# A 256-token hybrid decoder layer: low parts in whole blocks, one product moved forward, attention heads begun later

## The chip, the cores and the metric

The kernel runs on one NeuronCore of a Trainium2 chip. The core has a matmul engine (TensorE, PE in the rows; PEld is its loading of the stationary operand), a vector engine (VectorE, DVE), an activation engine (ScalarE, ACT), GpSimd (POOL) and SyncE (SP), which here only issues DMAs. The engines run side by side; each takes its own instructions in the order in which they were written and waits for the others through semaphores. The metric is the device time of one execution in microseconds (us).

## The reference, cut to what matters

One layer, 256 tokens, width 2048, float32. One wide projection feeds four causal attention branches of 4 heads each; every branch output is gated, projected, weighted with a sigmoid gate and summed; one output projection follows, then a norm.

```python
h = rms_norm(x, norm_w)
p = h @ w_in                     # (256, 2048) @ (2048, 17492)
(z, gate, dsa_qkv, idx_q, idx_k, idx_w, fox_qkv, fox_f, diff_qkv, dil_qkv) = jnp.split(p, IN_OFFSETS, axis=-1)
# four branches b, 4 heads of 128 each: softmax attention with a bias per head and pair of positions
#   0 top-k sparse (an indexer picks 64 keys), 1 forgetting, 2 difference of two softmaxes, 3 dilated
for b in range(N_BRANCHES):
    y = branches[b].reshape(bsz, seq, BRANCH_WIDTH) * jax.nn.silu(z_parts[b])
    term = jax.nn.sigmoid(g_parts[b]) * (y @ w_branch[b])
    merged = term if merged is None else merged + term
return x + merged @ w_out        # then a final rms_norm
```

## The kernel before, in words

**Numbers.** Every float32 operand of a matmul is split into a high part, rounded to the engine's faster float32 format, and a low part, the rest. One product of a 128x128 activation tile with 512 weight columns is three matmuls (`three`, L378 to L380): activation high by weight high, activation low by weight high, activation high by weight low.

**Units.** The weights pass through in units: a block of 512 rows by 512 columns (1 MB), loaded by SP into one of six raw slots. ACT copies it into `whi` (`split_hi`, L207), DVE subtracts into `wlo` (`split_lo`, L220), each in two halves of 128x1024, and PE runs 24 matmuls on it (12 where only one of the two 128-token halves is wanted). `whi` has 8 half buffers, `wlo` 6. The loop at the end of `body` writes the order: at each half of unit i it first writes the low part of the half that lies 5 halves ahead and the high part of the half that lies 7 ahead, then the unit's own matmuls. So when unit i ends, the low parts of two and a half later units have been written in DVE's queue, and the high parts of three and a half in ACT's. Only what stands behind them in a queue can be held up by them, and they by what stands ahead.

**Seven products.** A 2048 x 1024 stretch of `w_in` is done by `seven`: for one half of the rows (four blocks B11, B12, B21, B22) seven products P1 to P7 take the place of eight, with sums of blocks formed by DVE in place (`plus`, L187, three for each seven) and one by an accumulating DMA that POOL issues (`plus_dram`, L191: B12 + B11). P5 is the product that reads this accumulated sum. The other half of the rows is plain (units c2a, c2b, c1a, c1b). P units have 12 matmuls, c units 24. The order of the eleven units is a string: before, `P1 P3 P5 c2a P6 c2b P7 P2 c1a P4 c1b`. Four PSUM banks (X, Y, Z, W) take the sums; between products ACT and DVE read them out (classes `Tok` and `Gate`: p1, p5, u3 and c21 on ACT, u2, c12, c22 and c11 on DVE; in `Gate` a sigmoid on ACT follows). P5 goes alone into W, is read out by ACT (p5, L540), and only then may c2a write W again. c2a writes Z first (half of each half unit), then W.

**Stages.** After the indexer's projection come four branches, in the order 3, 2, 0, 1. A branch is: the seven of q and k (`ps_qk`), the seven of z and v (`ps_zv`), two sevens of gates (`ps_g`, called first and second gate here), and four units of the branch projection (`ps_b`). A merge and the output projection (`ps_o`) end the kernel.

**Threads.** The attention is written as generators that take one step after a unit, when enough units have passed (`pace`): `qk_thread` turns q and k on PE, `z_thread` forms silu(z) (a sigmoid on ACT, L625, and a product on DVE, L626) and turns it, `index_thread` scores and picks keys, and a `head_thread` or `diff_thread` for each of the 4 heads: logits on PE (L786), bias and maximum on DVE (L798 to L803), exponentials on ACT (L805); a step later the reciprocal on DVE; then the scaling on ACT (`scaled`, L821); then the transposes on PE (L812 to L814) with their copy `pt` on ACT (L816); one step later the product with v on PE (L876); then the output `y` and its high and low parts. The logits tile `lg` has three buffers, held from the logits until the transposes. Before, the four heads start with `qk_thread`, wait in `ready` until that has ended, and the first two (one for branch 2) go ahead while z and v are still being projected; the rest wait until `z_thread` has come to its turning. An instruction of a thread stands in its engine's queue between the `whi` or `wlo` of two units.

## Time and profile before

| | us |
|---|---|
| three runs, median (lowest to highest) | 1042.16 (1042.02 to 1044.82) |
| the profiled execution, its own time | 1044.16 |
| its span in the trace | 1042.4 |
| PE busy | 973.3 |
| DVE busy | 822.7 |
| ACT busy | 634.7 |
| mean granted clock of PE | 0.966 |

The span runs from the first to the last instruction of the trace; the time of the execution has 1.76 us more around it. A wait is put down to the engine and line that released it. "Idle before" in square brackets is the time in which the engine stood still ahead of that instruction. A granted clock of 1.00 is 2.4 GHz, 0.50 is 1.2 GHz. Stages are cut at the first matmul of each seven.

### The profile page before, as it was taken

How to read it: one execution, taken by the hardware profiler on the slowest of the kernel's cores; microseconds unless marked ns; L12 is line 12 of the kernel's file. 1: busy time of each engine (PE TensorE's matmuls, PEld its weight loads, DVE VectorE, ACT ScalarE, POOL GpSimd, SP SyncE). 2: the span in 40 equal slices, each digit the busy share in tenths (PEclk: the TensorE clock that was granted, in tenths of full speed). 3: DMA queues.
4: the chain of work that ended last, by engine and by line, in shares of the span. 5: the costliest groups of instructions: out<-in, count | busy, mean ns of one | idle time of the engine just before them, and what ended most of it. 6: DMA issues, size and time to landing. Idle time of an engine off the chain costs nothing. (4 is left out here: it accounts for less than half of the span.)

```text
span 1042.4 us, 12131 instructions
## 1 busy us (share of the span) xinstructions
PE 973.3 (93%) x4443; PEld 799.7 (77%) x4443; DVE 822.7 (79%) x967; ACT 634.7 (61%) x834; POOL 73.0 (7%) x84
## 2 busy tenths in 40 slices
PE   9988998999999989989999979799999797999897
PEld 8866886878878867778788858688788686887776
DVE  5888899978697877597888775887987767869992
ACT  5756676686456667676555665863666567544641
POOL 2011010000010000021100000001000000010220
PEclk9998999999999999989999989899999898999998
DMA  9949484747876938159895574388958562788132
GB/s 321 293 112 286 155 252 136 221 143 243 261 228 228 290 102 242 41 197 280 209 303 161 203 201 162 122 256 222 302 176 275 162 202 81 259 271 317 58 144 81
DMA packets 109019, 213.64 MB, mean 205 GB/s; under 512 B 8083, under 2 KB 10293, under 8 KB 108576
## 3 DMA queue, kind: packets, MB, share of 16 engines
q1 hardware_dynamic: 96240, 181.06, 50.1%
q0 software_dynamic: 12688, 31.80, 14.9%
q8 instruction: 35, 0.57, 0.2%
q14 instruction: 24, 0.20, 0.1%
q10 hardware_dynamic: 32, 0.01, 0.0%
HBM read 204.44 MB, written 8.41 MB: 204 GB/s over the span
## 5 line engine op out<-in xcount | busy, mean ns | idle before, releaser
L207 ACT ACTIVATE whi<-raw 128x1024 fp32r<-128x1024 f32 (+1 forms) x439 | 448.9, 1051 | 238.2 <-DVE raw L187 81.0
L220 DVE TENSOR_TENSOR wlo<-raw,whi 128x1024 fp32r<-128x1024 f32 (+1 forms) x439 | 525.6, 1224 | 84.3 <-PE ps_g L380 21.4
L378 PE MATMUL ps_g<-whi,hT 128*128 128x512 f32 x352 | 145.9, 415 | 25.9 <-ACT g L540 25.9
L380 PE MATMUL ps_g<-wlo,hT 128*128 128x512 f32 x352 | 141.9, 403 | 0.4 <-DVE wlo L220 0.4
L379 PE MATMUL ps_g<-whi,hT 128*128 128x512 f32 x352 | 142.2, 404 | 0.0
L187 DVE TENSOR_TENSOR raw<-raw 128x2048 f32<-128x2048 f32 x51 | 117.8, 2310 | 1.1
L378 PEld LDWEIGHTS ps_g<-whi,hT 128*128 128x128 f32 x352 | 69.6, 198 | 44.2 <-ACT g L540 28.4
L380 PEld LDWEIGHTS ps_g<-wlo,hT 128*128 128x128 f32 x352 | 69.1, 196 | 16.0 <-DVE wlo L220 0.8
L379 PEld LDWEIGHTS ps_g<-whi,hT 128*128 128x128 f32 x352 | 69.4, 197 | 14.0
L378 PE MATMUL ps_qk<-whi,hT 128*128 128x512 f32 x176 | 70.3, 399 | 6.9 <-ACT tok L540 6.9
L380 PE MATMUL ps_qk<-wlo,hT 128*128 128x512 f32 x176 | 69.5, 395 | 1.8 <-DVE wlo L220 1.8
L378 PE MATMUL ps_zv<-whi,hT 128*128 128x512 f32 x176 | 70.5, 400 | 0.5 <-ACT v L540 0.5
L379 PE MATMUL ps_qk<-whi,hT 128*128 128x512 f32 x176 | 69.6, 395 | 0.0
L380 PE MATMUL ps_zv<-wlo,hT 128*128 128x512 f32 x176 | 68.7, 390 | 0.0
L379 PE MATMUL ps_zv<-whi,hT 128*128 128x512 f32 x176 | 68.6, 390 | 0.0
L191 POOL DMA_DIRECT2D raw<-in_w_in_dram x16 | 21.1, 1316 | 503.5 <-DMA raw<-in_w_in_dram 191.1
L380 PE MATMUL ps_g<-wlo,sf 128*128 128x512 f32 x128 | 50.5, 395 | 2.3 <-DVE wlo L220 2.3
L378 PE MATMUL ps_g<-whi,sf 128*128 128x512 f32 x128 | 51.6, 403 | 0.0
L379 PE MATMUL ps_g<-whi,sf 128*128 128x512 f32 x128 | 50.3, 393 | 0.0
L378 PE MATMUL ps_b<-whi,yT 128*128 128x512 f32 x128 | 49.9, 390 | 0.0
L380 PE MATMUL ps_b<-wlo,yT 128*128 128x512 f32 x128 | 49.8, 389 | 0.0
L379 PE MATMUL ps_b<-whi,yT 128*128 128x512 f32 x128 | 49.8, 389 | 0.0
(266 smaller groups left out, 1567.3 us busy)
## 6 DMA issues: line engine op xcount, KB each, us to landing
raw<-in_w_in_dram SPq DMA_DIRECT2D x132, 1024.0 KB, 6.4
raw<-in_w_in_dram POOLq DMA_DIRECT2D x16, 1024.0 KB, 11.3
raw<-in_w_branch_dram SPq DMA_DIRECT2D x16, 1024.0 KB, 5.2
raw<-in_w_out_dram SPq DMA_DIRECT2D x16, 1024.0 KB, 5.8
md<-g POOLq DMA_DIRECT2D x12, 512.0 KB, 5.3
raw<-in_w_in_dram SPq DMA_DIRECT2D x7, 512.0 KB, 9.8
xs<-in_x_dram SPq DMA_DIRECT2D x8, 256.0 KB, 8.1
mp<-md POOLq DMA_DIRECT2D x4, 512.0 KB, 8.7
```

The costliest lines, as they stand in the source:

```text
L187: nc.vector.tensor_tensor(to.tile, of.tile, to.tile, op=op)
L191: nc.gpsimd.dma_start(to.tile.rearrange("p (k n) -> p k n", k=of.nk), of.src[of.k0 * P:(of.k0 + of.nk) * P, of.c0:of.c0 + of.n] .rearrange ...
L207: nc.scalar.activation(u.parts[0][h][:, s_], raw[:, s_], AF.Copy)
L220: nc.vector.tensor_tensor(u.parts[1][h][:, s_], raw[:, s_], u.parts[0][h][:, s_].bitcast(F32), op=ALU.subtract)
L378: nc.tensor.matmul(ps, ahi, u.hi(k)[:, cols], start=first, stop=False, skip_group_check=on)
L379: nc.tensor.matmul(ps, alo, u.hi(k)[:, cols], start=False, stop=False, skip_group_check=on)
L380: nc.tensor.matmul(ps, ahi, u.lo(k)[:, cols], start=False, stop=last, skip_group_check=on)
```

## The change

Five things are edited.

- `whi` and `wlo` become whole-block tiles (128x2048, 4 and 3 buffers: the same room). ACT still writes the high part in two halves; the low part of both halves is one DVE operation of 128x2048 (211 of them; the first units and the kept block of the end keep halves).
- The loop writes the high part of unit i+3 (both halves) and the low part of unit i+2 (at its first half) while unit i runs. When unit i ends, the low parts of two later units and the high parts of three stand in the queues.
- The order of a seven becomes `P1 P5 P3 c2a ...`; in the first one `P1 P2 P5 P3 c2a ...`.
- The head threads start together with `z_thread`, at the end of the z and v seven, whose last unit (c1b) now needs the q and k turning and the constants (and for branch 0 the indexer) to be done. Head h takes its first step 2h steps later than head 0. Between the transposes and the product with v stand two steps instead of one; in `diff_thread` one step less lies between the norm and its transposes.
- The pace of branch 2's last 22 units goes from 15 to 14.

```diff
 def split_hi ...
-                u.parts[0][h] = wp.tile([P, 1024], F32R, name="whi", tag="whi", bufs=HI)[:, :n_]
+                if h == 0:
+                    u.high = wp.tile([P, 2048], F32R, name="whi", tag="whi", bufs=HI // 2)
+                u.parts[0][h] = u.high[:, h * n_:(h + 1) * n_]
 def split_lo ...
+        both = kept is None and h == 1 and u.parts[1][0] is None
...
+        if both:
+            nc.vector.tensor_tensor(u.low[:, :2 * n_], u.raw.tile[:, :2 * n_],
+                                    u.high[:, :2 * n_].bitcast(F32), op=ALU.subtract)
+            parts = 0
 def seven ...
-              order="P1 P3 P5 c2a P6 c2b P7 P2 c1a P4 c1b", s0=0):
+              order="P1 P5 P3 c2a P6 c2b P7 P2 c1a P4 c1b", s0=0):
 def qkvz_units ...
-                      start=[("qk", qk_thread)] + start, **(dict(
-                          need={"P1": ["stack"], "P3": ["forms"]},
-                          order="P1 P2 P3 P5 c2a P6 c2b P7 c1a P4 c1b") if b == FIRST else {}))
+                      start=[("qk", qk_thread)], **(dict(
+                          need={"P1": ["stack"], "P5": ["forms"]},
+                          order="P1 P2 P5 P3 c2a P6 c2b P7 c1a P4 c1b") if b == FIRST else {}))
-                        "ps_zv", need={"c1b": ["qk"]}, start=[("z", z_thread)]))
+                        "ps_zv", need={"c1b": ["qk", "fox", "const"] + ["index"] * (b == 0)},
+                        start=[z_thread] + start))
 def head_thread ...   (diff_thread alike)
-        yield from ready(b, h, 2)
+        for _ in range(2 * h):
+            yield
...
-        yield from values(b)
         yield
         pt = transposed(e)
         yield
+        yield
         o = att_ps("o")
...
-            u.pace = 15 if b == 2 else 18
+            u.pace = 14 if b == 2 else 18
 def low ...
-        if i < len(units):
+        if i < len(units) and (h or kept(units[i]) is not None):
 main loop ...
             low(2 * i + h + LO - 1)
-            high(2 * i + h + HI - 1)
+            high(2 * i + h + HI - 2)
             u.mm(u, h)
```

What this moves, at three places. First, ACT's queue at the first gate of branch 0, from the read-out of P1 (L537) to just behind that of P5 (L540); `sg` is the sigmoid of z, `lg,sm` the exponentials of a head. Before:

```order
L537 ACTIVATE g<-ps_g,rst 128x512
L207 ACTIVATE whi<-raw 128x1024 x2
L821 ACTIVATE lg<-lg,sm 128x128
L821 ACTIVATE lg<-lg,sm 128x256
L805 ACTIVATE lg,sm<-lg,mx 128x128
L805 ACTIVATE lg,sm<-lg,mx 128x256
L625 ACT_TABLE_LOAD
L625 ACTIVATE sg<-tok 128x1024
L207 ACTIVATE whi<-raw 128x1024 x2
L540 ACTIVATE g<-ps_g,rst 128x512
```

The same place after (line numbers of the changed kernel are ten higher: L547 is p1, L550 p5, L635 the sigmoid, L815 the exponentials):

```order
L547 ACTIVATE g<-ps_g,rst 128x512
L209 ACTIVATE whi<-raw 128x1024 x2
L550 ACTIVATE g<-ps_g,rst 128x512
L635 ACTIVATE sg<-tok 128x1024
L815 ACT_TABLE_LOAD
L815 ACTIVATE lg,sm<-lg,mx 128x128
L815 ACTIVATE lg,sm<-lg,mx 128x256
L209 ACTIVATE whi<-raw 128x1024 x6
```

P5's read-out stood behind a scaling, two exponentials, a sigmoid with its table and four halves of `whi`; now two halves stand ahead of it. Second, DVE's queue at the same place, from z's last read-out (L562) on. Before (behind these rows come a head's bias and maximum, and only then z's product with its sigmoid, L626):

```order
L562 SCALAR_TENSOR_TENSOR tok<-ps_zv,rst,tok 128x512
L866 RECIPROCAL sm<-sm 128x2
L220 TENSOR_TENSOR wlo<-raw,whi 128x1024
L187 TENSOR_TENSOR raw<-raw 128x2048
L220 TENSOR_TENSOR wlo<-raw,whi 128x1024 x2
L187 TENSOR_TENSOR raw<-raw 128x2048
L220 TENSOR_TENSOR wlo<-raw,whi 128x1024
```

After, up to the same product (L636):

```order
L572 SCALAR_TENSOR_TENSOR tok<-ps_zv,rst,tok 128x512
L225 TENSOR_TENSOR wlo<-raw,whi 128x2048 x2
L187 TENSOR_TENSOR raw<-raw 128x2048
L636 TENSOR_TENSOR tok<-tok,sg 128x1024
```

The halves are gone, and a sum of blocks stands behind a whole low part. Third, ACT's queue at the end of the same first gate, from the sigmoid of c22 to the read-out of the second gate's P1. Before (`pt` is the copy of the transposes):

```order
L576 ACTIVATE g<-g 128x512
L207 ACTIVATE whi<-raw 128x1024 x2
L821 ACTIVATE lg<-lg,sm 128x128
L821 ACTIVATE lg<-lg,sm 128x256
L805 ACT_TABLE_LOAD
L805 ACTIVATE lg,sm<-lg,mx 128x128
L805 ACTIVATE lg,sm<-lg,mx 128x256
L207 ACTIVATE whi<-raw 128x1024 x4
L580 ACT_TABLE_LOAD
L580 ACTIVATE g<-g 128x512
L583 ACTIVATE g<-ps_g,rst 128x512
L816 ACTIVATE pt<-ptp 128x384 x3
```

After, the end of that stretch (L826 is `pt`, L831 the scaling, L590 the sigmoid of c11):

```order
L826 ACTIVATE pt<-ptp 128x384
L209 ACTIVATE whi<-raw 128x1024 x4
L590 ACT_TABLE_LOAD
L590 ACTIVATE g<-g 128x512
L593 ACTIVATE g<-ps_g,rst 128x512
L842 ACTIVATE yT<-y 128x256
L831 ACTIVATE lg<-lg,sm 128x128
L831 ACTIVATE lg<-lg,sm 128x256
L815 ACT_TABLE_LOAD
L815 ACTIVATE lg,sm<-lg,mx 128x128
L815 ACTIVATE lg,sm<-lg,mx 128x256
```

Three copies of transposes stood in a row; now one comes at a time, and a head's scaling and another head's exponentials stand behind the sigmoid of c11. Over the whole program ACT has 28 table loads instead of 30; no other count changes but that of the low parts.

## Rows read from the trace of the kernel before

**Rows 1.** The page, part 1: busy time, share and instructions of each engine.

```profile
PE 973.3 (93%) x4443; PEld 799.7 (77%) x4443; DVE 822.7 (79%) x967; ACT 634.7 (61%) x834; POOL 73.0 (7%) x84
```

**Rows 2.** Waits of PE, whole span: us in total, times, longest us.

```profile
PE ps_g L378 <- ACT g L540: 25.9, 6, 6.5
PE o L876 <- ACT pt L816: 14.6, 4, 6.7
PE ps_qk L378 <- ACT tok L540: 6.9, 4, 4.1
PE ps_qk L380 <- DVE wlo L220: 3.6, 3, 1.8
```

**Rows 3.** Windows by stage: length, busy of each engine (instructions), PEclk, DMA share, GB/s.

```profile
60.23:119.41 59.18, 51.56 (x233) 40.39 (x231) 49.98 (x70) 36.40 (x47) 3.34 (x5) 0.94 0.60 183
...
166.63:221.56 54.93, 49.33 (x220) 40.36 (x218) 47.71 (x93) 37.24 (x57) 1.34 (x1) 0.94 0.57 173
...
374.85:432.11 57.26, 52.17 (x225) 40.38 (x225) 40.38 (x70) 38.94 (x59) 1.30 (x1) 0.94 0.55 166
432.11:487.18 55.07, 49.40 (x213) 40.37 (x213) 44.92 (x58) 39.80 (x68) 9.90 (x9) 0.91 0.59 183
...
509.03:551.07 42.04, 41.10 (x181) 33.71 (x180) 36.02 (x30) 24.36 (x25) 2.98 (x3) 1.00 0.84 252
...
594.70:648.62 53.92, 47.41 (x210) 38.92 (x209) 34.46 (x43) 31.33 (x44) 1.29 (x1) 0.94 0.58 176
648.62:702.85 54.23, 47.16 (x202) 38.53 (x201) 44.59 (x49) 37.61 (x50) 1.29 (x1) 0.91 0.57 178
...
810.27:863.50 53.23, 47.50 (x210) 39.00 (x209) 33.07 (x40) 31.34 (x44) 1.28 (x1) 0.94 0.59 178
863.50:915.77 52.27, 45.70 (x202) 37.69 (x201) 43.75 (x46) 37.38 (x50) 0.00 (x0) 0.93 0.57 197
```

**Rows 4.** Windows, an even stretch and one behind a wait of PE.

```profile
240.00:250.00 10.00, 10.00 (x46) 8.29 (x45) 9.77 (x11) 5.24 (x8) 0.00 (x0) 1.00 0.64 223
...
611.60:616.60 5.00, 5.00 (x12) 3.94 (x13) 3.40 (x4) 1.93 (x2) 0.00 (x0) 0.50 1.06 218
```

**Rows 5.** Timeline, branch 0's first gate, ACT and PE: start, us, what [idle before].

```profile
606.71 1.28 ACT L625 ACT_TABLE_LOAD   x1
608.00 1.06 ACT L625 ACTIVATE sg<-tok 128x1024 f32<-128x1024 f32 x1
...
610.86 0.67 ACT L540 ACTIVATE g<-ps_g,rst 128x512 f32<-128x512 f32 x1
...
611.58 0.79 PE L378 MATMUL ps_g<-whi,hT 128*128 128x512 f32 x1 [6.51 <-ACT g L540]
```

**Rows 6.** Timeline, where branch 0's second gate begins: DVE, ACT and PE.

```profile
648.25 0.29 DVE L798 TENSOR_TENSOR lg<-lps,bias 128x128 f32<-128x128 f32 x1 [10.61 <-PE ptp L814]
...
656.05 1.28 ACT L580 ACT_TABLE_LOAD   x1
657.35 0.63 ACT L580 ACTIVATE g<-g 128x512 f32<-128x512 f32 x1
657.88 0.67 ACT L583 ACTIVATE g<-ps_g,rst 128x512 f32<-128x512 f32 x1
...
658.98 1.22 PE L876 MATMUL o<-pt,v 128*128 128x256 f32 x2 [6.72 <-ACT pt L816]
```

**Rows 7.** Timeline, PE in branch 0's q and k.

```profile
519.66 0.50 PE L378 MATMUL ps_qk<-whi,hT 128*128 128x512 f32 x1 [0.94 <-ACT tok L540]
```

**Rows 8.** Groups by line on DVE, and a pair of low halves in the timeline.

```profile
L220 DVE TENSOR_TENSOR wlo<-raw,whi 128x1024 fp32r<-128x1024 f32 (+1 forms) x439 | 525.6, 1224 | 84.3 <-PE ps_g L380 21.4 <-issue 20.5 <-PE ps_qk L380 11.0
L187 DVE TENSOR_TENSOR raw<-raw 128x2048 f32<-128x2048 f32 x51 | 117.8, 2310 | 1.1
...
649.80 2.35 DVE L220 TENSOR_TENSOR wlo<-raw,whi 128x1024 fp32r<-128x1024 f32 x2
```

**Rows 9.** Waits of ACT, whole span: us in total, times, longest us.

```profile
ACT whi L207 <- DVE raw L187: 81.0, 30, 5.1
```

More of the change, by code (lines that the diff above doesn't have):

```diff
@@ L210, in split_lo @@
         n_ = u.nk // 2 * u.n
+        both = kept is None and h == 1 and u.parts[1][0] is None
         if not part:
             if kept is None:
-                u.parts[1][h] = wp.tile([P, 1024], F32R, name="wlo", tag="wlo", bufs=LO)[:, :n_]
+                if h == 0 or both:
+                    u.low = wp.tile([P, 2048], F32R, name="wlo", tag="wlo", bufs=LO // 2)
+                for i in range(0 if both else h, h + 1):
+                    u.parts[1][i] = u.low[:, i * n_:(i + 1) * n_]
             else:
@@ L629, in z_thread @@
             V["sz"] = at.tile([P, 4, S], F32, name="sz", tag="sz")
-            V["v of"] = b
             yield from turn(z_, V["sz"], 0)
@@ L833, in put_y @@
         nc.vector.tensor_tensor(yT[:, h, 1], y, yT[:, h, 0].bitcast(F32), op=ALU.subtract)
-    def ready(b, h, early):
-        while any(a[0] in ("qk", "index", "fox", "const") for a in active):
-            yield
-        if h < early:
-            for _ in range(2 * h):
-                yield
-        else:
-            while V.get("v of") != b:
-                yield
-            for _ in range(h - early):
-                yield
-                yield
-    def values(b):
-        while V.get("v of") != b or any(a[0] == "z" for a in active):
-            yield
     def head_thread(b, h):
@@ L882, in diff_thread @@
             V["yT"] = big.tile([P, 4, 2, S], F32R, name="yT", tag="y")
-        yield from ready(b, h, 1)
+        for _ in range(2 * h):
+            yield
         er = []
@@ L899, in diff_thread @@
         yield
-        yield from values(b)
         yield
@@ L922, in diff_thread @@
                                     op0=ALU.mult, op1=ALU.mult)
-        yield
         yield
@@ L1248, in low @@
         i, h = divmod(q, 2)
-        if i < len(units):
+        if i < len(units) and (h or kept(units[i]) is not None):
             split_lo(units[i], h, kept(units[i]))
-    for q in range(2 * RAMP + 1, 2 * RAMP + HI - 1):
+    for q in range(2 * RAMP + 1, 2 * RAMP + HI - 2):
         high(q)
```

## The prediction

> **What bounds the kernel now.** I read the shares of the engines first. PE is busy 93% of the span [rows 1], and where it runs evenly its clock is the full one: 46 matmuls in 10.0 us, 0.22 us each [rows 4]. So what can be won is what PE loses: its idle time and the half clock behind it. DVE at 79% and ACT at 61% [rows 1] have room on average, but they bind place by place, which the next two views show.
>
> The waits of PE say for whom it waits. Most of it, 25.9 + 6.9 us, is c2a of a seven waiting until ACT has read P5 out of bank W; 14.6 us is the product with v waiting for the copy of the transposes on ACT; 3.6 us are low parts [rows 2]. The table by stage says where: PE's idle time, length less busy, is 7.62 us in the first q and k, 5.60 in branch 3's first gate, 5.09 and 5.67 in the gates of branch 2, 6.51 and 7.07 in those of branch 0, 5.73 and 6.57 in those of branch 1 [rows 3]: 49.9 us in eight stages. An undisturbed q and k loses 0.94 us [rows 3, 7], and there are three.
>
> Each long wait is paid twice. Behind the wait of 6.51 us the granted clock is 0.50 and 5.0 us hold 12 matmuls instead of 23 [rows 4]: 11 matmuls of 0.22, 2.4 us. The eight stages with idle time have granted clocks of 0.91 to 0.94, the undisturbed one 1.00 [rows 3].
>
> **Why PE waits there.** At the first gate of branch 0 P5's read-out on ACT starts at 610.86; ahead of it stand a table load and the sigmoid of z, from 606.71 [rows 5], and two exponentials that had waited for DVE. Seven microseconds went by in which ACT did other work first. Where the second gate begins DVE stood 10.61 us before a head's maximum [rows 6]: the fourth head's logits want one of three `lg` buffers, and the first head's transposes, which free it, are written a step and a whole c unit later on PE. Everything in DVE's queue behind it waits too, its lead is gone, and when it goes on, PE waits 6.72 us for copies that stand on ACT behind a sigmoid that waits for DVE [rows 6]. The same two waits stand in branch 1, with nearly the same lengths [rows 3].
>
> **The change, part by part.**
>
> *P5 second, P3 behind it.* No matmul is added. Between P5 and c2a's bank W now lie P3 (12 x 0.22 = 2.7 us) and the Z half of c2a's first half unit (1.3 us), and the read-out is written one unit earlier on ACT. In the three q and k without threads the 0.94 us end: 2.8 us. ACT also waited 81.0 us, 30 times, to round a block whose sum DVE had yet to form [rows 9]; of these the wait for P6's block goes, since P5's low part and the sum behind it are written a unit earlier and the high part half a unit later. In the first gates of branches 0 and 1 the threads step behind P5, so its read-out comes ahead of them, with two halves before it: 6.51 and 5.73 us go. In branches 2 and 3 the step falls behind P1, and the read-out still follows that step: sigmoid 1.06 [rows 5], z's product some 1.2, the head's maximum 1.0, a table load 1.28 [rows 5], exponentials 1.0, two halves 2.0, with P1's own read-out 0.7 and some gaps 9.2 us from P1's end. PE gets to bank W after 5.4 + 1.3 + 0.6 = 7.3. That leaves 1.9 us of the 5.09 in branch 2 (between 0, if ACT is early, and 5.1 as now), and some 4.5 of the 5.60 in branch 3, where `index_thread` puts 3 us more on DVE ahead of the product.
>
> *Heads with the gates, two steps apart.* The same steps are moved, none added; two table loads fewer. The ring of three `lg` buffers no longer holds in branches 0, 1 and 3: head 0's transposes come well before head 3's logits. So the 10.61 us of DVE and the 6.72 us behind it go, and the product with v has a step more between it and its copy. But now all four softmaxes lie in the gates. DVE's work in a first gate of branch 0 is then 11 low parts and 3 sums of 2.31 [rows 8], 5 read-outs of 0.75, four heads at 1.6 and some 3.4 us of small things: 45.5 us, against 40.8 us of PE (180 matmuls) and 4 of the heads on PE. ACT comes to about 43. Nothing is left over, and what one engine hands the other is waited for. The worst place by this count: the third head's transposes, one unit (P1) behind c1b. Its scaling stands on ACT behind a table load 1.28, the sigmoid of c11 0.63, c21's read-out 0.67 [rows 6] and 1.2 of scaling and `yT`; the sigmoid waits for DVE's read-out of c11 (0.75), which stands behind a low part and a sum (2 x 2.31, rows 8). If DVE has done these two when c1b ends, the scaling is ready after 4.5 us and PE, back there after 3.7, waits 0.8; if it has both before it, 9.1 and 5.4. I take 3.8, since ACT's own halves delay that low part. With 1.2 us at the head before and 1.5 at the next c2a: 6.5 us in branch 0 instead of 13.6, and 6 instead of 12.3 in branch 1, whose heads have one DVE operation less. Branch 2 has eight softmaxes, and there head 2's logits still want the buffer that head 0's transposes free, a unit later; I take 8 us (2 to 14) against 10.8.
>
> *Low parts in whole blocks.* A pair of halves is 2.35 us in a row, one after the other apart 2 x 1.224; a whole block should cost what the sum of the same size costs, 2.31 [rows 8]. 211 of them save DVE 8 to 29 us of its 822.7. PE gets that only where DVE is the bound, as in the first q and k with 49.98 of 59.18 [rows 3]. There I put 7.62 at 6 us (its low part now waits behind two more operations, its c2a no longer), and elsewhere nothing (0 to 4).
>
> *Half a unit less lead.* Each of PE's units now finds 2 low units and 3 high ones ahead instead of 2.5 and 3.5. In an even seven DVE has 36 of 42 us [rows 3] and covers it. The price shows where PE runs out of lead anyway: 1.4 us (half a P unit) to 2.7 (half a c unit) at a wait. I take 1 us at the end of the kernel; in the gates it is in the numbers above.
>
> **Sum.** Idle time 49.9 + 2.8 = 52.7 before; after: 6 + 4.5 + 8 + 6.5 + 6 = 31.0. That is 21.7 us less. Of about nine stretches at half clock four or five remain; 4 x 2.4 = 10 us less [rows 4]. Less 1 us at the end: 31 us. The profiled execution took 1044.16, 2.0 over the median of the runs. 1044.2 - 31 = 1013, against the median 1011 us.
>
> **Rivals.**
>
> *Most waits go* (985 or less to 997). If ACT and DVE meet their places a microsecond or two early, the remaining 31 us fall to 12 and only two half-clock stretches remain: 19 + 6 us more, 986. For it: DVE and ACT stood idle for 10 us in a row in branches 0 and 1, and that time comes back. Against it: the count of 45.5 us against 45.
>
> *The waits move* (1027 to 1042). The gates fill DVE to the brim, and branches 2 and 3 keep theirs: only the 2.8 us, the c2a waits of branches 0 and 1 (12.2) and two half-clock stretches (4.8) are won, and half of that is paid at new places: 1044 - 10 - 2 = 1032.
>
> *Coarse low parts with less lead* (slower). This is one mechanism: where DVE is late, PE gets the first half of a block only when the whole operation is done, and it had half a unit less in hand. PE's waits for low parts are 3.6 us in the first q and k [rows 2]; with 1.1 us (half an operation) and up to 2.7 (half a c unit) more at one place in each of the eight gates, and the half clock behind it (2.4), 8 x 5.3 = 42 us come, against the 31 won: 1055 - 2 = 1053. It decides when the waits for low parts pass some 35 us. Against it: DVE's waits for PE show that it is often early. The Trainium skill (Perfetto Trace Analysis, section Optimizing Scalar/DVE Operations) speaks for this rival: larger operations help where the engine is saturated, and where it is not but causes bubbles on others, breaking operations up lets work be done sooner; by its 60 ns for an operation of DVE on SBUF 211 fewer would save an estimated 13 us of DVE time. The trace has DVE at 79% with PE waiting for it, the second case of the rule, but the waits named are mostly ACT's.
>
> *It doesn't do what it says.* The accumulating DMA could be late for P5, now a unit earlier. ACT's order gives it several units in all sevens but the first, where P5's first half is wanted right behind it: no change or 3 us there.
>
> **Chances.** The forecast (997 to 1027): 0.55. Most waits go: 0.12. The waits move: 0.17, of it 0.04 within 0.3% of before. Slower: 0.13. Nothing of it: 0.03. The measurement of this kernel tells 0.3% (3 us) from no change. Faster 0.55 + 0.12 + 0.13 = 0.80; same 0.04 + 0.03 = 0.07; slower 0.13. The range from 985 to 1042 takes in the first three cases but their tails and leaves out the slower one.
>
> **What would show it.** In the changed profile: no wait of c2a for p5 in the q and k stages and in the first gates of branches 0 and 1; no wait of DVE for transposes above 3 us outside branch 2; the whole low part near 2.3 us; ACT's waits for sums well under 81 us; 25 to 35 us of idle PE time in gates and first q and k, now for scalings, copies and low parts. I am wrong if PE's waits for low parts grow past 35 us, or if the idle time of the gates stays near 42.

## The result, and the profile after

The changed kernel takes 984.89 us (median of three runs, 979.33 to 984.9) against 1042.16: a ratio of 0.9425, 95% interval 0.9371 to 0.948. The forecast was 1011, its range 985 to 1042: the median lies just below it, at the rival "Most waits go", whose sum was 986.

The profiled execution took 979.33 us, the shortest of the three, so the rows below stand 5.6 us under the median; where such a difference lies is told with the last experiments. Line numbers from L236 on are 10 larger in the changed kernel (L378 is L388), and 8 smaller behind the head threads (L1062 is L1054); the low part L220 is now L225 (the whole block) and L230 (halves), the high part L207 is L209. First the engines (part 1 of the page; answers rows 1) and the waits of PE (rows 2):

```profile
PE 952.4 (97%) x4443; PEld 788.6 (81%) x4443; DVE 800.9 (82%) x755; ACT 623.4 (64%) x832; POOL 79.0 (8%) x84
```

```profile
PE ps_g L390 <- DVE wlo L225: 6.3, 3, 2.8
PE ps_qk L390 <- DVE wlo L225: 4.9, 2, 4.3
PE ptp L822 <- ACT lg L831: 1.6, 1, 1.6
PE ps_o L388 <- DVE xf L1054: 1.4, 1, 1.4
```

The two largest lines of rows 2 are gone: no wait for P5's read-out (L550) and none for the copy `pt`. Low parts are what is left, 11.2 us. The span is 977.6, 64.8 us shorter, in two parts. PE is busy 20.9 us less with the same 4443 matmuls, so they ran faster on average (mean granted clock 0.966 before, 0.991 after). The other 43.9 us are idle time: 1042.4 - 973.3 = 69.1 before, 25.2 after (both with the edges of the span). The first part is the clock, row PEclk of part 2 of each page (40 slices, tenths of the full clock, 9 is 0.9 or more), before and then after:

```profile
PEclk9998999999999999989999989899999898999998
```

```profile
PEclk9999999999999999999999999999999999999999
```

The windows by stage answer rows 3 (length, busy of PE, PEld, DVE, ACT, POOL with instructions, granted clock, DMA share, GB/s): first q and k, branch 3's first gate, an undisturbed q and k, branch 2's gates, branch 0's gates.

```profile
60.35:116.08 55.73, 50.78 (x232) 40.39 (x231) 49.67 (x56) 35.62 (x45) 3.33 (x5) 0.94 0.61 190
162.53:216.21 53.68, 49.24 (x222) 40.10 (x221) 49.17 (x83) 41.58 (x63) 1.33 (x1) 0.97 0.59 177
...
280.68:321.48 40.80, 40.80 (x182) 33.80 (x180) 35.16 (x20) 23.75 (x25) 2.63 (x3) 1.00 0.82 258
364.24:415.84 51.60, 51.60 (x234) 39.81 (x232) 37.52 (x71) 39.42 (x72) 2.21 (x3) 1.00 0.61 184
415.84:466.52 50.68, 47.11 (x214) 38.17 (x212) 45.33 (x43) 36.15 (x59) 9.18 (x7) 0.97 0.59 173
571.81:617.40 45.59, 45.59 (x215) 38.09 (x214) 40.35 (x45) 37.59 (x54) 1.29 (x1) 1.00 0.68 208
617.40:661.12 43.72, 43.72 (x201) 36.43 (x199) 36.00 (x32) 32.48 (x46) 1.29 (x1) 1.00 0.69 216
```

In branch 0's gates, and in branch 1's alike, length and busy time agree: PE waits for nothing, at the full clock. Branch 0's two were 108.2 us together and are 89.3. DVE's and ACT's own waits (rows 6 and 9) went the same way: ACT stood 81.0 us before sums of DVE, now 19.5; DVE stood 23.3 + 10.6 us in all before logits for transposes, now 1.7. The three answers are ACT after, DVE before and DVE after:

```profile
ACT whi L209 <- DVE raw L187: 19.5, 7, 4.3
```

```profile
DVE lg L800 <- PE ptp L814: 23.3, 4, 10.6
...
DVE lg L798 <- PE ptp L814: 10.6, 1, 10.6
```

```profile
DVE lg L810 <- PE ptp L824: 1.7, 1, 1.7
```

### The profile page after: what moved, and what is told of

It reads as the page before. It is cut to its first block, busy times and chain, and to the rows that moved or that the text cites. A ratio compares the mean times of both kernels' runs of the same rounds, so it can differ in the third digit from the quotient of the medians.

```text
span 977.6 us, 11617 instructions
## 1 busy us (share of the span) xinstructions
PE 952.4 (97%) x4443; PEld 788.6 (81%) x4443; DVE 800.9 (82%) x755; ACT 623.4 (64%) x832; POOL 79.0 (8%) x84
## 4 chain that ended last, share of the span: by engine, by line
PE 81%; DVE 8%; ACT 4%; issue 3%; DMA 3%; POOL 0%; SPq 0%; POOLq 0%; ACTq 0%; DVEq 0%
PE ps_g L388 10%; PE ps_g L390 10%; PE ps_g L389 10%; PE ps_qk L390 5%; PE ps_qk L388 5%; PE ps_qk L389 5%; PE ps_zv L388 5%; PE ps_zv L389 5%; PE ps_zv L390 5%; DVE wlo L225 4%; PE ps_o L389 3%; PE ps_o L388 2%; PE ps_o L390 2%; PE ps_b L390 2%; PE ps_b L389 2%
## 5 line engine op out<-in xcount | busy, mean ns | idle before, releaser
L225 DVE TENSOR_TENSOR wlo<-raw,whi 128x2048 fp32r<-128x2048 f32 x212 | 484.8, 2294 | 60.3 <-issue 32.3
L209 ACT ACTIVATE whi<-raw 128x1024 fp32r<-128x1024 f32 (+1 forms) x439 | 437.0, 1048 | 141.5 <-issue 42.6
L390 PE MATMUL ps_g<-wlo,hT 128*128 128x512 f32 x352 | 138.1, 392 | 4.5 <-DVE wlo L225 4.5
L388 PE MATMUL ps_g<-whi,hT 128*128 128x512 f32 x352 | 141.0, 401 | 0.0
L389 PE MATMUL ps_g<-whi,hT 128*128 128x512 f32 x352 | 137.7, 391 | 0.0
L390 PEld LDWEIGHTS ps_g<-wlo,hT 128*128 128x128 f32 x352 | 66.4, 189 | 19.4 <-DVE wlo L225 5.3
L388 PEld LDWEIGHTS ps_g<-whi,hT 128*128 128x128 f32 x352 | 66.6, 189 | 15.1 <-issue 1.0
L389 PEld LDWEIGHTS ps_g<-whi,hT 128*128 128x128 f32 x352 | 66.6, 189 | 13.2
L388 PE MATMUL ps_zv<-whi,hT 128*128 128x512 f32 x176 | 69.6, 396 | 0.0
L388 PE MATMUL ps_qk<-whi,hT 128*128 128x512 f32 x176 | 68.7, 390 | 0.0
L389 PE MATMUL ps_qk<-whi,hT 128*128 128x512 f32 x176 | 68.6, 390 | 0.0
L388 PE MATMUL ps_g<-whi,sf 128*128 128x512 f32 x128 | 52.6, 411 | 0.0
L390 PE MATMUL ps_b<-wlo,yT 128*128 128x512 f32 x128 | 49.8, 389 | 0.0
L388 PE MATMUL ps_b<-whi,yT 128*128 128x512 f32 x128 | 49.8, 389 | 0.0
L389 PE MATMUL ps_b<-whi,yT 128*128 128x512 f32 x128 | 49.8, 389 | 0.0
```

The lines of the kernel that those rows point to most:

```text
L209: nc.scalar.activation(u.parts[0][h][:, s_], raw[:, s_], AF.Copy)
L225: nc.vector.tensor_tensor(u.low[:, :2 * n_], u.raw.tile[:, :2 * n_], u.high[:, :2 * n_].bitcast(F32), op=ALU.subtract)
L388: nc.tensor.matmul(ps, ahi, u.hi(k)[:, cols], start=first, stop=False, skip_group_check=on)
L389: nc.tensor.matmul(ps, alo, u.hi(k)[:, cols], start=False, stop=False, skip_group_check=on)
L390: nc.tensor.matmul(ps, ahi, u.lo(k)[:, cols], start=False, stop=last, skip_group_check=on)
```

## The experiments: one part alone, and all but one

The theory was that the waits lie at separate places and each part takes away its own; the rival, that the parts need one another.

**Order alone.** Only the strings are changed.

```diff
-              order="P1 P3 P5 c2a P6 c2b P7 P2 c1a P4 c1b", s0=0):
+              order="P1 P5 P3 c2a P6 c2b P7 P2 c1a P4 c1b", s0=0):
...
-                          need={"P1": ["stack"], "P3": ["forms"]},
-                          order="P1 P2 P3 P5 c2a P6 c2b P7 c1a P4 c1b") if b == FIRST else {}))
+                          need={"P1": ["stack"], "P5": ["forms"]},
+                          order="P1 P2 P5 P3 c2a P6 c2b P7 c1a P4 c1b") if b == FIRST else {}))
```

> The kernel before with P5 second and P3 behind it, in all sevens, and nothing else. Theory 'places': the change is a sum of waits at separate places, and each part takes away its own. The two groups of waits of c2a for P5 (25.9 + 6.9 us) go but for about 6 us in branches 2 and 3, and some four half-clock stretches at 2.4 us with them: 1042 - 27 - 10 = about 1005 (997 to 1015), with the waits of the product with v (14.6 us) still there. Rival 'parts need each other': ACT and DVE stay late through the old threads, so c2a finds another wait, and this alone gives under 12 us: 1030 or more.

Measured: 1021.75 us, ratio 0.9817 (0.9786 to 0.9848), between the two. **Heads alone** (the edits of `qkvz_units` without the strings, `head_thread`, `diff_thread` and the pace):

> The kernel before with the heads alone changed: they start with z's thread at the end of z and v, two steps apart, with a step more between the transposes and the product with v. Theory 'places': the 14.6 us of PE's waits of the product with v for the copy of the transposes go, with some four half-clock stretches at 2.4 us: 1042 - 14 - 9 = about 1019 (1012 to 1028); the c2a waits for P5 stay, or grow by some us as there are four heads in the gates. Rival 'parts need each other': the heads now all stand in the gates beside late read-outs, and the c2a waits grow by what the product's waits give: 1036 to 1050.

Measured: 1021.87 us, 0.982 (0.9785 to 0.9854), as the theory had it. **Whole blocks and the shorter lead alone** (the edits of `split_hi`, `split_lo`, `low` and the loop):

> The kernel before with whole-block low parts and half a unit less lead alone. Theory 'places': DVE gives back some 20 us, but PE waits on ACT, not on DVE's total, so little: 1036 to 1044. Rival 'coarse low parts with less lead': PE's waits for low parts grow from 3.6 us to 15 or more, with half-clock stretches behind them: 1055 or more. Rival 'DVE's time was the limit': the wins of all parts come from DVE's 20 us, and this alone gives over 15 us: 1027 or less.

Measured: 1020.46 us, 0.9809 (0.9779 to 0.9838). My theory fell here: the part that I had taken for nothing gives 20 us, as much as either other. The waits of PE in the three, order, heads and whole blocks:

```profile
PE o L876 <- ACT pt L816: 18.8, 4, 8.0
PE ps_g L380 <- DVE wlo L220: 6.0, 3, 3.3
PE ps_g L378 <- ACT g L548: 4.8, 3, 2.1
```

```profile
PE ps_g L378 <- ACT g L540: 26.1, 8, 5.5
PE ps_qk L378 <- ACT tok L540: 6.9, 4, 4.0
```

```profile
PE ps_g L390 <- DVE wlo L225: 16.6, 7, 4.8
PE ps_g L388 <- ACT g L550: 11.9, 2, 6.4
PE o L886 <- ACT pt L826: 7.0, 2, 4.3
```

Order ends the waits for P5 (L540, 25.9 + 6.9 us before, nearly all gone) but the product with v waits 4 us longer, and c1a now waits for u3's read-out (L548). Heads leave P5 as it was and end the other line, but for a wait of 2.7 us for the copy in branch 2, whose product has another tile (`od`). Whole blocks cut both, and bring waits for low parts: 19.0 us with the first q and k against 6.3.

Then all parts but one. Without the order, and without the heads:

> The changed kernel with the old order of products (P3 second, P5 third; in the first q and k P3 ahead of P5). Theory 'places': the waits of c2a for P5 come back, at least the 0.94 us in three q and k, 6.5 and 5.7 in the first gates of branches 0 and 1 and some 2 to 5 each in branches 2 and 3, with about five half-clock stretches: 985 + 25 + 12 = 1022 (1010 to 1030). Rival 'the heads took ACT's work away from there': with all parts but this one the read-out of P5 is in time in most places, and it stays under 1000.

> The changed kernel with the old start and spacing of the heads (order and whole blocks as in the change). Theory 'the parts add': 985 + 19 = 1004 (998 to 1009); the waits of the product with v for the copy of the transposes are back in branches 0 and 1, some 7 us each with low parts in it. Rival 'order and place suffice': with ACT in time the ring of logits costs less, 995 or less.

Measured: 1004.08 us, 0.9642 (0.9609 to 0.9674), and 1016.64, 0.9734 (0.9698 to 0.977). Without whole blocks, with the old lead:

> The changed kernel with half low parts and the old lead (order and heads as in the change). Theory 'the parts add': 985 + 20 = 1005 (999 to 1010), with ACT's waits for sums back near 60 us. Rival 'they hang together': without whole blocks the heads in the gates find no time on DVE, and it is above 1015.

Measured: 995.07 us, 0.9556 (0.9534 to 0.9579). None of these three lies in the range that separate places gave (1010 to 1030, 998 to 1009, 999 to 1010). Stage by stage, from the windows of the profiled executions (us; gates are the two of a branch together):

| stage | before | order | heads | whole | no order | no heads | no whole | after |
|---|---|---|---|---|---|---|---|---|
| first q and k | 59.2 | 65.2 | 59.3 | 55.0 | 55.9 | 59.2 | 65.4 | 55.7 |
| other q and k, three | 126.2 | 122.4 | 126.2 | 124.4 | 124.4 | 122.4 | 122.4 | 122.4 |
| gates, branch 3 | 99.4 | 102.8 | 98.3 | 97.4 | 97.3 | 99.1 | 97.9 | 96.4 |
| gates, branch 2 | 112.3 | 100.7 | 112.0 | 103.2 | 107.7 | 103.7 | 101.1 | 102.3 |
| gates, branch 0 | 108.2 | 102.0 | 99.3 | 107.3 | 98.3 | 104.6 | 89.3 | 89.3 |
| gates, branch 1 | 105.5 | 99.5 | 97.1 | 105.8 | 97.3 | 101.5 | 89.3 | 89.3 |
| output projection | 103.2 | 101.1 | 102.6 | 97.9 | 98.1 | 98.3 | 103.0 | 98.5 |

The three parts alone save 18.7, 18.6 and 20.0 us against 1040.46, the median of before measured beside them: 57.3 in all, and the change saves 57.3. Taken away from the whole they are not alike: by the ratios the order is worth 0.022 (23 us) behind the others, the heads 0.031 (32), whole blocks 0.013 (14). By stages they overlap and need each other. Branches 0 and 1 need order and heads, and with these two they are free of waits without whole blocks. In branch 2 order or whole blocks does it alone (100.7 and 103.2), but beside the moved heads whole blocks without the order leave 107.7. With whole blocks the first q and k takes 55.0 to 59.2 us and the output projection 97.9 to 98.5, without them 59.2 to 65.4 and 101.1 to 103.2. And with the order alone the first q and k is 6 us longer.

## The experiments: what in "whole blocks" gave 20 us

The part holds three things: one operation for two, the low part of a first half written half a unit later, and high parts written half a unit later. High parts later, alone:

```diff
-    for q in range(2 * RAMP + 1, 2 * RAMP + HI - 1):
+    for q in range(2 * RAMP + 1, 2 * RAMP + HI - 2):
...
-            high(2 * i + h + HI - 1)
+            high(2 * i + h + HI - 2)
```

This moves one thing more. The sum for P7's block (B11 less B12) is written on DVE by the same call, so it too stands half a unit later, and its high part is as far behind it as before. The two were not tried apart.

> The kernel before with one edit: the high part of a half is written half a unit later, six halves ahead of PE instead of seven, with the same eight half buffers; low parts stay halves at their old places, nothing else changes. Theory 'place': the 20 us of whole blocks alone came from ACT, which no longer stands before a sum of DVE (81.0 us in 30 waits before, 41.2 in 17 with whole blocks) nor before PE for a buffer (37.0 + 44.2 + 28.6 us before): then this alone gives most of it, 1024 to 1032. Rival 'one operation': they came from DVE's shorter work and its low part standing in one piece beside the sum; then this gives under 4 us: 1037 or more, or slower by the missing lead.

Low parts as two half operations at the place of the second, alone:

```diff
-        if i < len(units):
+        if i < len(units) and (h or kept(units[i]) is not None):
+            if h and units[i].parts[1][0] is None:
+                split_lo(units[i], 0)
             split_lo(units[i], h, kept(units[i]))
```

> The kernel before with the low parts of both halves of a block written at the place of the second, as two operations one behind the other; high parts stay at their old places. Theory 'place' (of the high parts): nothing, 1036 to 1046. Rival 'one operation': DVE's half operations in pairs already save part of it (the pair 2.35 us against 2 x 1.228): 1027 to 1036. Rival 'less lead': slower, 1048 or more, with longer waits for low parts.

Both together, which is the part but for the one operation:

> Both edits: low parts in pairs of halves at the place of the whole operation, high parts half a unit later; this is the part with whole blocks but for the whole operation itself. Theory 'place': within 5 us of the run with whole blocks alone (1020.5): 1018 to 1026. Rival 'one operation': 1032 or more, the difference to 1020 being what the whole operation gives.

Measured: high parts later 1023.95 us, 0.9831 (0.9808 to 0.9853); low parts in pairs 1050.6, 1.0097 (1.0064 to 1.013); both 1019.14, 0.9788 (0.976 to 0.9816). So the place of the high part, with P7's sum, carries it. By stages its gain lies in branch 2's gates (112.3 to 104.5 us), the three other q and k (126.2 to 122.4), the first q and k (59.2 to 56.4) and the output projection (103.2 to 101.2); the gates of branch 0 keep their 108.1, those of branch 1 their 105.7. The place of the low part by itself costs 8 us; once the high parts are later it costs nothing, and the output projection is 2.8 us shorter with it (98.4 against 101.2). The whole operation, with its whole-block tiles, gives nothing: 1020.46 against 1019.14, though DVE is busy 801.0 us with it and 815.2 with pairs.

What the place does is seen in an undisturbed q and k, ACT in branch 0's (rows 7 is the wait of PE in it), before and with high parts later:

```profile
513.50 1.06 ACT L207 ACTIVATE whi<-raw 128x1024 fp32r<-128x1024 f32 x1 [3.43 <-DVE raw L187]
514.47 0.67 ACT L537 ACTIVATE tok<-ps_qk,rsth 128x512 f32<-128x512 f32 x1
515.04 3.99 ACT L207 ACTIVATE whi<-raw 128x1024 fp32r<-128x1024 f32 x4
518.94 0.67 ACT L540 ACTIVATE tok<-ps_qk,rst 128x512 f32<-128x512 f32 x1
```

```profile
497.20 0.69 ACT L537 ACTIVATE tok<-ps_qk,rsth 128x512 f32<-128x512 f32 x1 [1.89 <-PE ps_qk L380]
498.72 3.91 ACT L207 ACTIVATE whi<-raw 128x1024 fp32r<-128x1024 f32 x4 [0.83 <-DVE raw L187]
502.64 0.69 ACT L540 ACTIVATE tok<-ps_qk,rst 128x512 f32<-128x512 f32 x1
```

Before, the high part of P6 stands in ACT's queue ahead of P1's read-out, and the sum that it rounds has only just been written to DVE's. ACT stands 3.43 us, and everything behind it moves: P5's read-out comes 9.9 us after the stage's first matmul (509.03), now 8.4 (494.28), and PE's 0.94 us are gone. P4's block stands in the same position, right behind the sum for it, in the old order and in the new. Counted block by block in the traces, the 81.0 us before sums are 31.3 us before P6's block (12 times), 45.0 before P4's (15) and 4.6 before others. The order alone leaves 1.5 before P6's and 49.8 before P4's; high parts later alone leave 10.0 and 16.1, and 7.8 before P7's, where it was 3.7. How much of this is PE's time differs by place: with order and heads but the old lead ACT still stands 42.7 us before P4's block, and PE waits for nothing in the gates of branches 0 and 1.

The later place leaves a half buffer of eight unused, so that ACT no longer needs the one that PE has just freed. To tell the two apart, the same with seven buffers:

```diff
-... name="whi", tag="whi", bufs=HI)[:, :n_]
+... name="whi", tag="whi", bufs=HI - 1)[:, :n_]
```

> The kernel before with the high part half a unit later (as in the run with that edit alone, 1024), but with seven half buffers instead of eight, so that ACT again needs the buffer that PE's last half unit has freed. Theory 'sum': what counts is that the high part is no longer written right behind the sum that it rounds: 1022 to 1028. Rival 'buffer': what counted was the spare buffer, ACT not being held to PE's pace: 1036 or more.

Measured: 1024.45 us, 0.9824 (0.9786 to 0.9862), as with eight. ACT waits for buffers again, at no cost in time; before sums it waits 24.8 us instead of 81.0:

```profile
ACT whi L207 <- PE ps_g L379: 37.4, 36, 3.4
...
ACT whi L207 <- DVE raw L187: 24.8, 19, 4.2
```

## The experiments: the ring of logits, and what would be better

The buffer saved leaves room for a fourth `lg`; the fourth was not tried on the kernel before alone. Order and heads are those of before.

```diff
-        lg = at.tile([P, 384], F32, name="lg", tag="lg", bufs=3)
+        lg = at.tile([P, 384], F32, name="lg", tag="lg", bufs=4)
```

> The same with a ring of four buffers for the logits instead of three; the heads stay where they were. Theory 'ring': DVE's wait of 10.6 us for the transposes goes in branches 0 and 1, and with it PE's waits of 6.7 and 6.6 us for the copy and the half clock behind them: 13 + 2 x 2.4 = 18 us below the run with three (12 to 20). Rival 'copy behind the sigmoid': the product with v still stands one step behind its copy, which ACT makes behind a sigmoid that waits for DVE: under 5 us, with waits of 4 us and more for the copy still there.

Measured: 995.85 us, 0.9543 (0.9514 to 0.9572): 28.6 us below the run with three buffers, more than the 12 to 20 expected. The three-buffer run's waits for the ring and behind it, of DVE and of PE:

```profile
DVE lg L800 <- PE ptp L814: 16.8, 3, 9.1
...
DVE lg L798 <- PE ptp L814: 8.8, 1, 8.8
```

```profile
PE o L876 <- ACT pt L816: 14.7, 4, 6.8
```

With four buffers none of these lines is left, and P5's remain:

```profile
PE ps_g L378 <- ACT g L540: 15.8, 6, 6.5
```

The gates of branches 0 and 1 go from 106.8 and 105.3 us to 97.0 and 97.4, and those of branch 2 from 105.9 to 97.3, which my expectation had left out. One part with halves remained: order and heads with high parts later, low parts at their old places.

> Order and heads as in the change, the high part half a unit later, but the low parts as halves at their old places with their old lead. Theory 'place': the whole operation itself gives nothing, so this is within 4 us of the changed kernel (985), with fewer of its 11.2 us of waits for low parts: 978 to 988. Rival 'one operation': DVE's 20 us more are felt now that it is the busiest next to PE: 990 to 996, little under the run without whole blocks (995).

Measured: 989.53 us, 0.9477 (0.9443 to 0.9512), between the two expectations; its interval overlaps that of the changed kernel. Then the order on top of four buffers, without and with the moved heads, with pairs of halves, and the changed kernel beside them on the same chip:

> The kernel before with three edits: P5 second, the high part half a unit later (seven half buffers), four buffers for the logits. Heads at their old places, low parts as halves at their old places. Theory 'ring': all that the moved heads give is that the first head's buffer is free in time, so with four buffers the old heads do as well as the new: 996 - 20 for the order = 976 (972 to 983), below the changed kernel. Rival 'spacing': with P5 early the old heads' products meet their copies late again, and waits of the product with v of 3 us and more are there: 986 or more.

> The same with the heads of the change too. Theory 'ring': within 4 us of the run without them; what is left of it is branch 2, whose third and fourth heads still want a buffer that transposes free: its second gate 50.7 us long in the changed kernel, 46.1 with four buffers. 972 to 981. Rival 'spacing': 6 us or more below the run with the old heads.

> The same again, with low parts as pairs of halves at the place of the whole operation. Theory 'place': the end of the kernel, w_out, takes some 98.4 us with the pairs against 101 with the halves at their old places, and PE's waits for low parts in the gates grow by 2 to 4: within 3 us of the run before it. Rival 'less lead': 5 us or more above it.

> The changed kernel once more, on the same chip as the three above, so that they can be compared: 985 (979 to 988).

Measured: 994.24 us, 0.9542 (0.9502 to 0.9582); 986.89, 0.9471 (0.9431 to 0.9511); 979.67, 0.9406 (0.9367 to 0.9446); the changed kernel 983.5, 0.9441 (0.9394 to 0.9488). The theory that four buffers replace the moved heads fell: the moved heads still give 7.4 us. They win 6.8 in the gates of branches 0 and 1 (93.8 and 91.9 us without them, 89.7 and 89.3 with them) and 3.4 in the z and v stages, and lose 6.3 in the gates of branches 2 and 3, 3.9 us in all. Another 3.4 us lie in the first q and k (59.9 against 58.5) and the output projection (101.4 against 99.4), where no head stands, so how much of the 7.4 the heads themselves give is open. Without them, P7's read-out and the copy are late again (waits of PE):

```profile
PE ps_g L378 <- ACT g L548: 5.4, 3, 2.6
...
PE o L876 <- ACT pt L816: 3.5, 3, 2.4
```

The order that was to save 20 us on top of four buffers saved next to nothing (0.9542 against 0.9543): it won 8.6 in the gates of branches 0 and 1, and lost 4.2 in the first q and k (59.9 against 55.7) and 2.3 in the gates of branch 3. With the moved heads beside it, pairs of halves save 7.2 more, though neither expectation had them faster by more than 3: branch 3's gates go from 100.6 to 95.9 us and branch 2's from 100.4 to 97.8, while the first q and k grows from 58.5 to 61.5. That kernel is 3.8 us below the changed one.

The first q and k was left. In the runs so far it took 54.6 to 65.4 us with P5 ahead of P3, and 55.0 to 56.4 with P3 ahead wherever high parts were later.

```diff
-                          need={"P1": ["stack"], "P5": ["forms"]},
-                          order="P1 P2 P5 P3 c2a P6 c2b P7 c1a P4 c1b") if b == FIRST else {}))
+                          need={"P1": ["stack"], "P3": ["forms"]},
+                          order="P1 P2 P3 P5 c2a P6 c2b P7 c1a P4 c1b") if b == FIRST else {}))
```

> Order, heads, pairs of half low parts, high part half a unit later with seven half buffers and four buffers for the logits (979.7 in the run above), but with the old order in the first q and k alone (P3 ahead of P5). Theory 'late load': there P5 second has its low part and the sum ahead of P3's low part, so that the next block's buffer comes free and its load starts some 3 us later; ACT then stands 8 us before that load and PE 3.7 us for the read-out behind it. With the old order there the first q and k takes 55 to 56.5 us instead of 61.5 and the whole 974 to 977. Rival 'no order there is better': the wait of c2a for P5 of 3.1 us comes back and the sum stays within 2 us of 979.7.

> The kernel of 979.7 once more, on the same chip as the run before: 978 to 982.

Measured: 976.07 us, 0.9365 (0.9341 to 0.939), and beside it 979.74, 0.939 (0.9364 to 0.9415). Windows of the first q and k, P3 ahead and then P5 ahead:

```profile
59.88:115.59 55.71, 50.71 (x233) 40.20 (x232) 50.78 (x68) 35.67 (x46) 3.34 (x5) 0.94 0.61 190
```

```profile
60.11:122.02 61.91, 53.15 (x232) 41.74 (x231) 51.06 (x68) 35.78 (x46) 3.34 (x5) 0.92 0.55 171
```

ACT's waits for loads of weights from 60 to 120 us, in the same order:

```profile
ACT whi L207 <- DMA raw<-in_w_in_dram: 4.0, 1, 4.0
```

```profile
ACT whi L207 <- DMA raw<-in_w_in_dram: 11.9, 2, 8.0
```

The stage is 6.2 us shorter, the median 3.7. Branch 3's gates and the output projection give back 2.4 of it (97.3 and 99.3 against 95.9 and 98.3). The wait for a load is shown; that P5's low part and sum, ahead of P3's low part, are what frees the buffer later is argued, not shown. In this stage executions of the changed kernel differ too: 55.7 us in the profiled one, where ACT waits 6.0 us for loads, and 58.2 in that of the repeat, where it waits 11.4. The repeat's span is 4.0 us longer (981.6); another 1.7 of that lie in branch 3's gates (98.1 against 96.4). The version of 976 us beats both kernels. It has the change's order but for the first seven, its heads, high parts half a unit later in seven buffers, pairs of half low parts, and four buffers of logits.

## Why the prediction was wrong

Most of the waits were named rightly; the sum was half of what came. The steps that failed are the 12.5 us of new waits in the gates of branches 0 and 1, where none came, and the later high part, priced as a loss where it gave 18 us by itself. Idle time of the stages in the sum: 52.7 us before, 31.0 forecast, 13.0 measured. Clock: 10 forecast, 20.9 measured. Of the 43.9 us of idle time, 3.1 lie in the output projection (13.8 to 10.7) and 0.9 in branch 3's second gate, which the sum did not have as gains. Term by term, from the windows:

| term | before | forecast | after |
|---|---|---|---|
| first q and k | 7.6 | 6 | 4.95 |
| three q and k | 2.8 | 0 | 0 |
| branch 3's first gate | 5.6 | 4.5 | 4.44 |
| branch 2's gates | 10.8 | 8 | 3.57 |
| branch 0's gates | 13.6 | 6.5 | 0 |
| branch 1's gates | 12.3 | 6 | 0 |

**P5 second: right in its places.** The waits for P5 go in the q and k and in the first gates of branches 0 and 1, as [rows 5] was read. In branch 3, 4.44 meets the 4.5 by luck: it is no wait for P5 any more but one for a low part (2.8) and one for a scaling (1.6). In branch 2's first gate nothing is left of the wait for P5, where 1.9 us were forecast. What the step left out is the first q and k, where the order by itself is worse (65.2 against 59.2): "its c2a no longer" came with 15.1 us of ACT's waits for loads in that stage, 5.1 before. That the order makes these loads late is argued.

**The ring: right.** [rows 6] gave the cause, and a fourth buffer, on top of later high parts and without any moved head, took those waits away in all three branches. That branch 2's head 2 would "still want the buffer" was right, but at the new spacing the wait is 1.7 us. How the new spacing alone ends the waits in branches 0 and 1 was not separated from the later start.

**The new waits in branches 0 and 1: the mis-sized term.** The 12.5 us came from a count of 45.5 us of DVE against 45 of PE; the items as listed make 45.9. The stage shows DVE at 40.35 in 45.59 us. The large items were right: 11 low parts and 3 sums are 32.0 us by their groups. But I added durations, and these overlap: three DVE operations in a row of the changed kernel,

```profile
623.53 2.29 DVE L225 TENSOR_TENSOR wlo<-raw,whi 128x2048 fp32r<-128x2048 f32 x1 [0.36 <-ACT whi L209]
625.74 2.28 DVE L187 TENSOR_TENSOR raw<-raw 128x2048 f32<-128x2048 f32 x1
627.94 2.28 DVE L225 TENSOR_TENSOR wlo<-raw,whi 128x2048 fp32r<-128x2048 f32 x1
```

start 2.21 and 2.20 us apart. Of the 45 operations 26 start before the one ahead has ended, 0.08 us each, 2.1 us in all: the durations sum to 42.5. The other 3 us were counted and are not there: only three of the four heads' maxima lie in this stage, and the small things are about 2 us, not 3.4. So DVE is ahead, not at the brim. The place named as the worst, the third head's transposes behind P1 of the second gate, shows it (DVE, ACT and PE; c1b's last matmul starts at 616.71):

```profile
611.75 2.29 DVE L225 TENSOR_TENSOR wlo<-raw,whi 128x2048 fp32r<-128x2048 f32 x1 [0.45 <-ACT whi L209]
614.08 2.29 DVE L187 TENSOR_TENSOR raw<-raw 128x2048 f32<-128x2048 f32 x1
616.29 0.74 DVE L572 SCALAR_TENSOR_TENSOR g<-ps_g,rst,g 128x512 f32<-128x512 f32 x1
...
613.55 1.28 ACT L590 ACT_TABLE_LOAD   x1
617.07 0.63 ACT L590 ACTIVATE g<-g 128x512 f32<-128x512 f32 x1 [2.23 <-DVE g L572]
...
618.48 0.79 ACT L831 ACTIVATE lg<-lg,sm 128x128 f32<-128x128 f32 x2
...
620.99 0.27 PE L822 MATMUL ptp<-ident,lg 128*128 128x128 f32 x1
```

Low part and sum are done when c1b ends; the read-out of c11 (L572) starts ahead of that end, since its bank is complete six matmuls earlier; and ACT has loaded its table while it waited. The scaling ends at 619.27, 2.2 us behind c1b's end and not 4.5, and the transposes start 1.7 us later. The prediction had this case (0.8 us of wait) and the bad one (5.4) and took 3.8, nearer the bad one, on the count. It does not need whole blocks: without them both branches' gates have the same 89.3 us.

**Half a unit less lead: wrong in sign.** It was priced as a loss (1 us at the end, the rest in the gates), and whole blocks at nothing but in the first q and k. [rows 9] had the gain in it: ACT stood 81 us before sums. I took away the wait for P6's block, 31.3 us of it, under the order. I did not see that 45.0 stand before P4's block, where the order changes nothing and the later high part by itself leaves 16.1, nor that by itself it also cuts P6's, to 10.0. Alone the later high part gives 18 us, on top of order and heads 8 by the ratios (0.9477 against 0.9556), and the whole part 14. The end of the kernel was to be 1 us worse and is 4.7 better (98.5 against 103.2).

**The half clock: right in kind, half in size.** 2.4 us a stretch and four or five stretches fewer made 10. Most went, and the 4443 matmuls took 20.9 us less. The size follows the idle time: 20.9 to 43.9, about what 10 to 21.7 was.

**The slower rival.** Its mechanism is in the runs: low parts written later cost 8 us by themselves (1050.6) with waits for low parts grown from 6.3 to 17.2 us (the low parts in pairs, alone),

```profile
PE ps_g L380 <- DVE wlo L220: 12.9, 6, 3.7
...
PE ps_qk L380 <- DVE wlo L220: 4.3, 3, 2.2
```

but not to 35, and later high parts pay for it. What the Trainium skill says (Perfetto Trace Analysis, section Optimizing Scalar/DVE Operations) is borne out on both sides. Larger operations saved DVE 14.2 us (815.2 less 801.0), where its 60 ns gave an estimated 13. Operations broken up let PE go on sooner, with 12.9 us of waits for low parts for pairs at the same places and 19.0 for whole blocks. The time is the same with both (1020.46 and 1019.14 us).

**Chances.** "Most waits go" had 0.12, held down by the count of DVE. Its idle time, 12 us left, came close (13.0). That its 986 came so close to 984.89 is in part luck: its clock was 16 us against 20.9, and the gain in the output projection was not in it.

## What to carry to other kernels

When an in-order engine rounds, copies or reads out for several consumers, look for the instruction in its queue that stands right behind the one it needs on another engine: writing it half a unit later gave 18 us here, though it shortened a lead. A ring that is one buffer short shows as an engine that waits for a consumer far downstream; try one buffer more, and if room is lacking look for a ring with one to spare, before work is moved. Whether an engine is full is better counted from start to start of its operations in a row: the sum of their durations was 2.1 us over its busy time here, in a stage of 45.6.

## What the runs showed that I had not expected

DVE operations of 128x2048 in a row start 0.08 us before the one ahead has ended (2.28 us long, 2.20 apart), so sums of durations overstate a busy engine. A buffer for ACT's high parts that it had to wait for 37.4 us in the gates alone cost nothing (1024.45 against 1023.95): a wait of an engine that is ahead was no loss here. And gains of three separate edits, 57 us, added up to the whole almost exactly. That is chance: stage by stage they overlap in branch 2 and need each other in branches 0 and 1, and taken away from the whole they are worth 23, 32 and 14 us.
